# Attention's low parts on VectorE, and the output gate's sums behind each step's own work, in a gated attention and mLSTM layer

## The chip, the core and the metric

The kernel runs on one core of one Trainium2 chip. The metric is the device time of one execution in microseconds (us). The kernel before took 353.72 us, the median of three runs (353.52 to 354.63). TensorE (PE) multiplies matrices; VectorE (DVE), ScalarE (ACT) and GpSimd (POOL) work element by element; SyncE (SP) issues most of the transfers. Each engine works through its own queue in program order and waits where an operand isn't ready.

## The reference, cut to what matters

One layer with 256 tokens and width 1024, all in fp32:

```
ada = c @ w_ada + b_ada;  shift, scale, gate = split(ada, 3)
h  = rmsnorm(x, norm_w) * (1 + scale) + shift
qa ka va za qm km vm zm om ig fg ga gm = split(h @ w_in)
ya = (attention(rmsnorm(qa), rmsnorm(ka), va) * silu(za)) @ w_att_proj
qm, km = silu(causal_conv(qm, km))
hm = rmsnorm(sigmoid(om) * mlstm(qm, km, vm, ig, fg))
ym = (hm * silu(zm)) @ w_ml_proj
y  = sigmoid(ga) * ya + sigmoid(gm) * ym
out = x + gate * (y @ w_out)
```

With 256 tokens the attention has one block and is plain causal attention with a bias.

## The kernel before, in words

**Three passes per product.** PE multiplies in float32r. To keep fp32's precision each operand is split in two: a high part, which ScalarE rounds (`wh`, `hTh`, `yah`, `ymh`), and a low part, the difference, which is a subtraction (`wl`, `hTl`, `yal`, `yml`). PE then makes high by high, high by low and low by high. So every weight that PE uses costs ScalarE one rounding of 128x1024 (L451) and VectorE or GpSimd one subtraction of 128x1024 (L455).

**The stages.** A first stage normalizes x and makes the columns q and part of k. Then one loop over 118 steps does the rest. A step is two of a matrix's eight blocks of 128 input rows, for 512 output columns. The steps are, by the first of each half: ka 0, va 4 and 8, za 12 and 16, qm 20 and 24, zm 28, km 42 and 46, att (attention's projection) 50 and 54, vm 58, ga 72 and 76, om 80, gm 94 and 98, ml (the mLSTM's projection) 102 and 106, out 110 and 114. zm, vm and om have 14 steps and are made by Strassen's scheme with seven products: sums of weight blocks (`sum_forms`) are made before and beside them on VectorE and by accumulating DMAs that POOL issues. A sum may be written over a block (L497), once both subtractions that read the block are done.

**The order in step g** is written out by hand. First the weights of step g+4 are split (`split`, L439 to 456): ScalarE rounds, then VectorE subtracts, or POOL in the ten steps of `pool_lo`, among them 28, 29 (issued at steps 24, 25) and 103, 104 (issued at 99, 100). The ring of `wh` and `wl` has five buffers (HB, L432), so a rounding waits until PE is through with the step five before. Then, at the first step of a chunk, the chunk before is read out of PSUM. Then follow the hooks of the step, in the order in which `at` registered them. Last come PE's matmuls.

**Attention's output.** `att_av` (L746) multiplies probabilities by values for two heads and VectorE multiplies by silu(za) into `yf`; `att_split` (L762) rounds it on ScalarE (`yah`) and subtracts on POOL (`yal`). Heads 4 to 7 have their products at step 22 and their splitting at step 23. PE uses `yah` and `yal` from step 50.

Also at steps 20 to 27: `left_split` and `left_low` (L516, L520) split sums of h for the Strassen products, `sum_forms(zm, 3)` at step 23 issues a DMA from POOL's queue (L481) that adds into the block of zm's weights, `conv` (L778) at steps 24 and 25 reads qm, and `sum_forms(zm, 2)` (L497) at the same steps writes over the block that steps 28 and 29 have read.

**mLSTM's output, steps 94 to 104.** `ml_num` (L870) makes a head's numerator: matmuls, VectorE's product with sigmoid(om) (L883), ScalarE's absolute value and square (L884, L886). `ml_y` (L888) makes the factor of two heads with four small VectorE and three small POOL instructions (L893 to 899). `ml_y2` (L902) multiplies four pieces by it and by silu(zm) (L908). `ml_T` (L911) transposes the result on PE (L919) and splits it into `ymh` (ScalarE, L923) and `yml` (VectorE, L924), which step 102 multiplies. They stand at steps 94, 95, 97 (`ml_num`), 96, 97 (`ml_y`), 97, 98 (`ml_y2`), 99, 100 (`ml_T`).

**The gates.** `ga_mult` (L833) multiplies sigmoid(ga) with attention's projection in halves. `ev_gm` (L837) puts sigmoid(gm) into the same buffer (slot s4) that holds attention's projection. The output gate of `ada` is made by eight sums, `gate_acc` (L942, L944), over weights that `gate_load` brings in four transfers; `gate_write` and `gate_read` (steps 106, 109) spread it over the partitions, for the last read-out (`ev_out`).

A tiny matmul of 128x8 (L1139) stands in five places that `EXTRA` (L301) lists.

Of the kernel before, what the change touches and what calls it, by code (L numbers as in the profile page):

```python
# [9 lines left out]
F32 = mybir.dt.float32  # L10
F32R = mybir.dt.float32r
AF = mybir.ActivationFunctionType
OP = mybir.AluOpType
# [51 lines left out]
def tile_hybrid(ctx: ExitStack, tc: tile.TileContext, x, c, params, params2, rel_t, w_row, ada_mod, ada_gate,  # L65
                w_in, w_att_proj, w_ml_proj, w_out, out):
    nc = tc.nc
# [191 lines left out]
    def some(*what):  # L259
        return lambda k: [mm_row(k, ch, (i,)) for ch, i in what]  # L260
# [19 lines left out]
    for step in P1_STEPS:  # L280
        op, k = step[0], int(step[1])
        if op == "L":
            next_loads(k)
        else:
# [9 lines left out]
                 e=some((0, 0), (0, 1), (0, 2), (1, 0), (1, 1), (1, 2), (2, 0), (2, 1), (3, 0), (3, 1), (2, 2), (3, 2))  # L294
# [3 lines left out]

    chunks = []

    EXTRA = (('za', 0, 0), ('qm', 0, 2), ('km', 0, 0), ('ga', 0, 0), ('ml', 0, 0))  # L301
    STRASSEN = ('zm', 'vm', 'om')

    def seg(kind, src, c0, name, stat=None):
# [29 lines left out]
    def start(name, half=0):  # L334
        return step0[C[name, half]]

    def done(name, half):
        return step0[C[name, half]] + (14 if name in STRASSEN else 4)
# [89 lines left out]
    def aux(shape):  # L428
        return ps.tile(shape, F32, name="aux", bufs=4)
# [5 lines left out]
    for nm, hf in (("qm", 0), ("qm", 1), ("km", 0), ("km", 1)):  # L435
        s = (start("km") if (nm, hf) == ("qm", 1) else done(nm, hf)) + 4
# [23 lines left out]
    def at(step, fn, *a):  # L460
        hooks.setdefault(step, []).append((fn, a))
# [4 lines left out]
    T = {}  # L466
# [295 lines left out]
    def att_split(h0):  # L762
        yf, hs = T["yf", h0], slice(h0, h0 + 2)
        nc.scalar.copy(T["yah"][:, hs], yf)
        nc.gpsimd.tensor_tensor(T["yal"][:, hs], yf, T["yah"][:, hs].bitcast(F32), op=OP.subtract)


    def ev_va(pt, half):
# [226 lines left out]
    for nm in ("qm", "km"):  # L995
        for hf in range(2):
            s = done(nm, hf)
# [4 lines left out]
    for q in range(2):  # L1002
        at(done("za", 0) + 1 + q, att_av, 2 * q)
        at(done("za", 1) + 2, att_av, 4 + 2 * q)
        at(done("za", 0) + 2 + q, att_split, 2 * q)
        at(done("za", 1) + 3, att_split, 4 + 2 * q)
    s = done("km", 0)
    s = done("km", 1)
    at(s + 3, ml_scores, 0)
# [3 lines left out]
    at(start("zm") + 4, gate_init, 0)  # L1013
    at(start("om") - 2, gate_init, 1)
    at(done("ga", 0) + 1, ga_mult, 0)
    at(start("gm") + 5, ga_mult, 1)
    for q, (nm, i, j, k) in enumerate((("km", -9, 4, 6), ("gm", -9, 1, 2), ("ml", -4, -2, -1), ("ml", -3, 0, 2))):
        s = start(nm)
        at(s + i, gate_load, q)
        at(s + j, gate_acc, 2 * q)  # L1020
        at(s + k, gate_acc, 2 * q + 1)
    at(start("ml") + 4, gate_write)
# [6 lines left out]
    for nm in STRASSEN:  # L1029
        s = start(nm)  # L1030
# [8 lines left out]
    for hp in range(2):  # L1039
        s = done("om", hp)  # L1040
        if "om" in STRASSEN:
            for i in range(2):
                at(s + (2 * i + 1, i)[hp], ml_num, 2 * hp + i)
                at(s + (6, 5)[hp], ml_T, 2 * hp + i)
            at(s + (3, 2)[hp], ml_y, hp)
            at(s + (4, 3)[hp], ml_y2, hp)
            continue
        at(s + 1, ml_num, 2 * hp)
        at(s + 2, ml_num, 2 * hp + 1)
        at(s + 3, ml_y, hp)  # L1050
        at(s + 4, ml_y2, hp)
        at(s + 8, ml_T, 2 * hp)
        at(s + 8, ml_T, 2 * hp + 1)

    A = HB - 1
    cons = {}
# [20 lines left out]
    for g in range(NG):  # L1077
# [36 lines left out]
        if ch["kind"] == "str":  # L1114
            p = kp // 2
            o = mmt[ci][(0, 2, 0, 1, 0, 2, 0)[p]]
            for kk in range(2):
                k = 2 * (kp % 2) + kk
# [5 lines left out]
        for kk in range(2):  # L1124
            k = 2 * kp + kk
# [8 lines left out]
            else:  # L1134
                for i in range(4):
                    cs = slice(i * 128, (i + 1) * 128)
                    o = mmt[ci][:, i]
                    if i == 0 and kk == 0 and (ch["name"], ch["half"], kp) in EXTRA:
                        nc.tensor.matmul(aux([128, 8]), wh[:, 0, cs], sh_[:, k, 0:8], start=True, stop=True)  # L1139
# [63 lines left out]
```

## Time and profile before

| | |
|---|---|
| median of three runs | 353.72 us |
| the profiled execution | 353.89 us |
| its span | 352.1 us |
| ScalarE busy | 236.6 us (67%) |
| VectorE busy | 291.3 us (83%) |
| GpSimd busy | 90.9 us (26%) |
| HBM read | 81.89 MB |
| granted TensorE clock | 1.00 throughout |

The span is the profiled execution from its first to its last instruction; 1.8 us lie around it. Times in the profile's timelines count from the span's start. A row of a timeline gives the start, the duration, the engine, the line of the kernel, the operation, what it writes and reads, how many instructions were merged into the row, and in brackets how long the engine had been idle before it and what released it. PE's matmuls are pipelined: they start every 0.11 to 0.24 us, but each lasts longer, so PE's time is read from the starts.

### The profile page before, as it was taken

The numbers are of one execution on the slowest core, as the hardware profiler recorded it, in microseconds if no ns is written. First come the engines' busy times: TensorE is split into PE (matmuls) and PEld (weight loads), VectorE is DVE, ScalarE is ACT, GpSimd is POOL, SyncE is SP. The second block draws the span as 40 slices with busy tenths as digits, with TensorE's granted clock in tenths as the row PEclk, the third lists the DMA queues.
The fourth block names the chain that finished last, engine by engine and source line by source line (L and its number), as shares of the span: only waits on it lengthen the run. The fifth ranks groups of instructions, "written<-read, shape, count | busy, mean of one in ns | idle before, by whom it ended". The sixth has DMA issues, their size and how long they took to land.

```text
span 352.1 us, 6030 instructions
## 1 busy us (share of the span) xinstructions
PE 342.8 (97%) x2313; PEld 312.5 (89%) x2313; DVE 291.3 (83%) x419; ACT 236.6 (67%) x366; POOL 90.9 (26%) x92
## 2 busy tenths in 40 slices
PE   7999999999999999899999999999999999999995
PEld 4987889888999999688999998899988998899885
DVE  3899995898988877999786899998988877698772
ACT  3776787989886946679688657866497554754410
POOL 3940003775101628001453272001000023500000
PEclk9999999999999999999999999999999999999999
DMA  7999999995567699097760973929969369066011
GB/s 275 411 419 421 419 385 345 237 248 240 187 196 280 98 368 236 16 334 323 248 231 2 352 194 63 393 80 360 274 216 400 120 225 374 2 218 202 0 61 60
DMA packets 29534, 83.72 MB, mean 238 GB/s; under 512 B 2109, under 2 KB 5185, under 8 KB 28994
## 3 DMA queue, kind: packets, MB, share of 16 engines
q1 hardware_dynamic: 26944, 78.08, 61.2%
q0 software_dynamic: 2112, 4.19, 7.2%
q10 hardware_dynamic: 450, 1.07, 0.9%
q8 instruction: 18, 0.29, 0.3%
q14 instruction: 10, 0.08, 0.1%
HBM read 81.89 MB, written 1.45 MB: 237 GB/s over the span
## 4 chain that ended last, share of the span: by engine, by line
PE 70%; DVE 10%; DMA 8%; POOL 4%; ACT 3%; issue 3%; SPq 0%; DVEq 0%; POOLq 0%; ACTq 0%
PE mm L1140 13%; PE mm L1142 13%; PE mm L1143 13%; DMA raw<-in_w_row_dram 8%; DVE wl L455 5%; PE pm L186 4%; PE aux L1121 4%; PE aux L1120 4%; PE aux L1122 4%; POOL ms L593 2%; PE mm L1132 2%; PE mm L1131 2%; PE mm L1133 2%; ACT wh L451 1%; PE mm L1154 1%
## 5 line engine op out<-in xcount | busy, mean ns | idle before, releaser
L455 DVE TENSOR_TENSOR wl<-raw,wh 128x1024 fp32r<-128x1024 f32 (+1 forms) x96 | 116.0, 1235 | 19.9 <-ACT wh L451 19.8
L451 ACT CAST wh<-raw 128x1024 fp32r<-128x1024 f32 (+1 forms) x106 | 107.2, 1032 | 28.1 <-PE mm L1142 22.3
L1140 PE MATMUL mm<-hTh,wh 128*128 128x256 f32 x320 | 89.9, 281 | 0.0
L1142 PE MATMUL mm<-hTl,wh 128*128 128x256 f32 x320 | 88.9, 278 | 0.0
L1143 PE MATMUL mm<-hTh,wl 128*128 128x256 f32 x320 | 88.8, 278 | 0.0
L1140 PEld LDWEIGHTS mm<-hTh,wh 128*128 128x128 f32 x320 | 60.3, 188 | 0.1
L1143 PEld LDWEIGHTS mm<-hTh,wl 128*128 128x128 f32 x320 | 60.3, 188 | 0.0
L1142 PEld LDWEIGHTS mm<-hTl,wh 128*128 128x128 f32 x320 | 60.1, 188 | 0.0
L455 POOL TENSOR_TENSOR wl<-raw,wh 128x1024 fp32r<-128x1024 f32 x10 | 25.4, 2606 | 47.2 <-ACT wh L451 47.2
L1131 PE MATMUL mm<-wh,hTh 128*128 128x512 f32 (+1 forms) x64 | 23.8, 372 | 0.0
L1133 PE MATMUL mm<-wh,hTl 128*128 128x512 f32 (+1 forms) x64 | 23.2, 363 | 0.0
L1132 PE MATMUL mm<-wl,hTh 128*128 128x512 f32 (+1 forms) x64 | 23.2, 363 | 0.0
L1121 PE MATMUL aux<-wl,Sh 128*128 128x512 f32 x48 | 19.0, 396 | 1.2 <-DVE wl L455 1.2
L175 DVE TENSOR_TENSOR wrl<-raw,wrh 128x512 fp32r<-128x512 f32 (+1 forms) x24 | 18.2, 780 | 1.1 <-ACT wrh L170 0.8
L1120 PE MATMUL aux<-wh,Sh 128*128 128x512 f32 x48 | 18.7, 390 | 0.0
L1122 PE MATMUL aux<-wh,Sl 128*128 128x512 f32 x48 | 18.7, 389 | 0.0
L1142 PE MATMUL mm<-yml,wh 128*128 128x256 f32 x64 | 17.8, 278 | 0.3 <-DVE yml L924 0.3
L1140 PE MATMUL mm<-yah,wh 128*128 128x256 f32 x64 | 17.8, 279 | 0.0
L170 ACT CAST wrh<-raw 128x512 fp32r<-128x512 f32 (+1 forms) x24 | 15.8, 684 | 3.0 <-DMA raw<-in_w_row_dram 3.0
L1140 PE MATMUL mm<-ymh,wh 128*128 128x256 f32 x64 | 17.8, 277 | 0.0
L1142 PE MATMUL mm<-yal,wh 128*128 128x256 f32 x64 | 17.7, 276 | 0.0
L1143 PE MATMUL mm<-yah,wl 128*128 128x256 f32 x64 | 17.7, 276 | 0.0
(247 smaller groups left out, 815.6 us busy)
## 6 DMA issues: line engine op xcount, KB each, us to landing
raw<-in_w_in_dram SPq DMA_DIRECT2D x36, 1024.0 KB, 7.3
adat<-in_ada_mod_dram SPq DMA_DIRECT2D x16, 512.0 KB, 9.4
gw<-in_ada_gate_dram SPq DMA_DIRECT2D x4, 1024.0 KB, 8.7
raw<-in_w_att_proj_dram SPq DMA_DIRECT2D x4, 1024.0 KB, 8.1
raw<-in_w_ml_proj_dram SPq DMA_DIRECT2D x4, 1024.0 KB, 4.9
raw<-in_w_out_dram SPq DMA_DIRECT2D x4, 1024.0 KB, 4.9
raw<-in_w_row_dram SPq DMA_DIRECT2D x4, 896.0 KB, 12.1
raw<-in_w_in_dram POOLq DMA_DIRECT2D x3, 1024.0 KB, 9.9
```

Source lines behind the costliest of these rows:

```text
L175: e.tensor_tensor(l[:, cs], wrow[k][:, cs], h[:, cs].bitcast(F32), op=OP.subtract)
L451: nc.scalar.copy(h, w)
L455: e.tensor_tensor(l, w, h.bitcast(F32), op=OP.subtract)
L1120: nc.tensor.matmul(o, a, wh[:, kk], start=k == 0 and p in (0, 1, 3), stop=False, skip_group_check=True)
L1121: nc.tensor.matmul(o, a, wl[:, kk], start=False, stop=False, skip_group_check=True)
L1122: nc.tensor.matmul(o, b, wh[:, kk], start=False, stop=k == 3, skip_group_check=True)
L1131: nc.tensor.matmul(o, a, wh[:, kk], start=first, stop=False)
L1132: nc.tensor.matmul(o, a, wl[:, kk], start=False, stop=False)
L1133: nc.tensor.matmul(o, b, wh[:, kk], start=False, stop=last)
L1140: nc.tensor.matmul(o, wh[:, kk, cs], sh_[:, k], start=first and i % 2 == 0, stop=False, skip_group_check=True)
L1142: nc.tensor.matmul(o, wh[:, kk, cs], sl_[:, k], start=False, stop=False, skip_group_check=True)
L1143: nc.tensor.matmul(o, wl[:, kk, cs], sh_[:, k], start=False, stop=last and i % 2 == 1, skip_group_check=True)
```

## The change

Three edits.

First, heads 4 to 7 of attention's output are split at step 22, right behind their product, and their low parts are subtracted by VectorE and no more by POOL. The tiny matmul of qm moves from step 22 to step 23.

Second, the second half of `ga_mult` moves from step 99 to step 94.

Third, the gate's sums 2 to 7 are registered after all other hooks of their step, and some move: sum 2 stays at step 95, 3 goes from 96 to 101, 4 from 100 to 101, 5 from 101 to 102, 6 from 102 to 103, 7 stays at 104. Sums 0 and 1 and all the loads stay.

```
-    EXTRA = (('za', 0, 0), ('qm', 0, 2), ('km', 0, 0), ('ga', 0, 0), ('ml', 0, 0))
+    EXTRA = (('za', 0, 0), ('qm', 0, 3), ('km', 0, 0), ('ga', 0, 0), ('ml', 0, 0))
...
         nc.scalar.copy(T["yah"][:, hs], yf)
-        nc.gpsimd.tensor_tensor(T["yal"][:, hs], yf, T["yah"][:, hs].bitcast(F32), op=OP.subtract)
+        e = nc.gpsimd if h0 < 4 else nc.vector
+        e.tensor_tensor(T["yal"][:, hs], yf, T["yah"][:, hs].bitcast(F32), op=OP.subtract)
...
         at(done("za", 0) + 2 + q, att_split, 2 * q)
-        at(done("za", 1) + 3, att_split, 4 + 2 * q)
+    for q in range(2):
+        at(done("za", 1) + 2, att_split, 4 + 2 * q)
...
-    at(start("gm") + 5, ga_mult, 1)
-    for q, (nm, i, j, k) in enumerate((("km", -9, 4, 6), ("gm", -9, 1, 2), ("ml", -4, -2, -1), ("ml", -3, 0, 2))):
+    for q, (nm, i, j, k) in enumerate((("km", -9, 4, 6), ("gm", -9, 1, 7), ("ml", -4, -1, 0), ("ml", -3, 1, 2))):
         s = start(nm)
         at(s + i, gate_load, q)
+        if q:
+            continue
         at(s + j, gate_acc, 2 * q)
         at(s + k, gate_acc, 2 * q + 1)
...
+    at(start("gm"), ga_mult, 1)
+    for s, j in ((start("gm") + 1, 2), (start("gm") + 7, 3), (start("gm") + 7, 4), (start("ml"), 5),
+                 (start("ml") + 1, 6), (start("ml") + 2, 7)):
+        at(s, gate_acc, j)
```

## The prediction

> **What bounds the kernel now.** I read the page first, then PE's waits, then the chain of waits and each engine's timeline around the two places that the waits point to.
>
> ```profile
> span 352.1 us, 6030 instructions
> PE 342.8 (97%) x2313; PEld 312.5 (89%) x2313; DVE 291.3 (83%) x419; ACT 236.6 (67%) x366; POOL 90.9 (26%) x92
> ```
>
> PE is the bound: 97% of the span, with no piece of its work added or taken away here. So the change can only win what PE stands idle, and lose where it makes PE idle. PE's waits, longest in total first (line that waited, what released it: total, times, longest):
>
> ```profile
> PE aux L1121 <- DVE wl L455: 1.2, 2, 0.6
> PE aux L1120 <- DVE pq L545: 0.6, 1, 0.6
> PE aux L1139 <- ACT ymh L923: 0.5, 1, 0.5
> ...
> PE aux L919 <- DVE omt L908: 0.4, 1, 0.4
> PE mm L1142 <- DVE yml L924: 0.3, 1, 0.3
> PE aux L919 <- ACT wh L451: 0.3, 1, 0.3
> ```
>
> Two stages stand here: zm's Strassen products (L1120, L1121; 1.8 us in three waits) and the way from mLSTM's output into its projection (L919, L1139, L1142; 1.5 us in four waits). An idle row understates a loss, since each matmul's end is modelled. PE's timeline, three matmuls of zm:
>
> ```profile
> 146.36 0.40 PE L1122 MATMUL aux<-wh,Sl 128*128 128x512 f32 x1
> 146.59 0.40 PE L1120 MATMUL aux<-wh,Sh 128*128 128x512 f32 x1
> 147.59 0.49 PE L1121 MATMUL aux<-wl,Sh 128*128 128x512 f32 x1 [0.61 <-DVE wl L455]
> ```
>
> Undisturbed, one starts 0.23 us after the other; here it took 1.00, a loss of 0.77 where the row says 0.61, so 0.16 more. With 0.16 for each wait, zm loses 1.8 + 3 x 0.16 = 2.3 us and the mLSTM stage 1.5 + 4 x 0.16 = 2.1 us: 4.4 us is the most that can be won.
>
> **Attention's splitting and zm.** What it moves: two roundings of ScalarE and two subtractions go forward a step, and the subtractions go from POOL to VectorE. POOL's queue, then ScalarE's, then VectorE's, from their timelines:
>
> ```profile
> 129.98 3.52 POOL L765 TENSOR_TENSOR yal<-yf,yah 128x512 fp32r<-128x512 f32 x2 [9.83 <-ACT yah L764]
> 133.44 1.33 POOL L481 DMA_DIRECT2D raw<-in_w_in_dram  x1
> 134.27 5.30 POOL L455 TENSOR_TENSOR wl<-raw,wh 128x1024 fp32r<-128x1024 f32 x2
> ```
>
> ```profile
> 131.15 1.05 ACT L451 CAST wh<-raw 128x1024 fp32r<-128x1024 f32 x1 [0.73 <-ACT yah L764]
> 132.11 1.01 ACT L789 ACTIVATE qmT<-mm,prm 128x256 f32<-128x256 f32 x2
> 133.99 1.05 ACT L451 CAST wh<-raw 128x1024 fp32r<-128x1024 f32 x1 [0.87 <-PE mm L1142]
> ```
>
> ```profile
> 126.30 0.68 DVE L522 TENSOR_TENSOR Sl<-lsum,Sh 128x512 fp32r<-128x512 f32 x1
> 129.41 1.23 DVE L455 TENSOR_TENSOR wl<-raw,wh 128x1024 fp32r<-128x1024 f32 x1 [2.44 <-ACT wh L451]
> 130.56 1.79 DVE L522 TENSOR_TENSOR Sl<-lsum,Sh 128x512 fp32r<-128x512 f32 x1
> 133.15 2.43 DVE L795 SCALAR_TENSOR_TENSOR qmT<-mm,prm,qmT 128x255 f32<-128x255 f32 x6 [0.81 <-ACT qmT L789]
> 137.24 3.42 DVE L497 TENSOR_TENSOR raw<-t,raw 128x1024 f32<-128x1024 f32 x1 [1.66 <-POOL wl L455]
> ```
>
> The two subtractions hold POOL until 133.50, then comes its DMA issue, and only at 134.27 the two weight subtractions of steps 28 and 29, whose roundings were ready at 132.20 and 135.04. VectorE's sum L497, which overwrites that block, must wait for the first of them (idle 1.66), and then it takes 3.42 us, of which only the last 1.09 lie behind the end of POOL's second subtraction at 139.57: it was held while POOL ran. The same is seen in L522, 1.79 us beside POOL and 0.68 without.
>
> After the change POOL is free long before 132.20. Its first weight subtraction runs from 132.20 and its second from 135.04, where PE's release of the ring (the 0.87 in ScalarE's row) puts the rounding. A subtraction that nothing disturbs is in the row of step 103, from POOL's timeline:
>
> ```profile
> 299.15 2.40 POOL L455 TENSOR_TENSOR wl<-raw,wh 128x1024 fp32r<-128x1024 f32 x1 [4.98 <-ACT wh L451]
> ```
>
> So the first ends at 134.60 and the second at 137.44 (at the mean of the pair, 2.65, at 137.69). L497 still stands behind the second, as VectorE comes to it at 135.58, and ends at 138.53 to 138.78 where it ended at 140.66: VectorE is 1.9 to 2.1 us ahead. I take 2.0. What that is worth is decided by whether VectorE has any other idle time up to PE's last wait there:
>
> ```profile
> 148.60 9.16 DVE L455 TENSOR_TENSOR wl<-raw,wh 128x1024 fp32r<-128x1024 f32 x8
> ...
> 160.55 0.67 DVE L545 TENSOR_TENSOR pq<-pq,aux 128x512 f32<-128x512 f32 x1
> ```
>
> It has none: eight subtractions back to back, no idle time in brackets, up to L545, which released PE's third wait. So the 2.0 us pass through to PE, out of 2.3 lost; the first two waits go and 0.3 stays at L545. **First term: -2.0.**
>
> Its costs: the two subtractions on VectorE, 2 x 0.68 (L522 has the same shape), lie in the 2.44 us of idle time ahead of 129.41. If that cover were gone they would cost at most their 1.36. ScalarE's two roundings now stand ahead of `left_split` and of step 27's rounding; that is ordering inside the same idle time, at nothing. The DMA of POOL's queue (L481, at 133.44) moves forward too, to about when POOL's earlier work ends; it asks for nothing that is made in between, and what it collides with is a rival below. The tiny matmul is one either way: nothing, within ±0.25 (about the spacing of one matmul).
>
> **The gate and the mLSTM stage.** The chain of waits shows where the path runs there (start, the piece's share of the path):
>
> ```profile
> 286.50 1.20 DVE gw L944
> ...
> 294.21 1.68 DVE omt L908 x4
> 295.89 1.15 DVE gat L835
> ...
> 302.41 1.19 DVE gw L944
> ```
>
> and ScalarE's and PE's timelines:
>
> ```profile
> 297.12 1.03 ACT L840 ACTIVATE gmt<-mm 128x1024 f32<-128x1024 f32 x1 [5.25 <-DVE gat L835]
> ```
>
> ```profile
> 291.94 0.30 PE L919 MATMUL aux<-ident,omt 128*128 128x128 f32 x1 [0.26 <-ACT wh L451]
> ...
> 296.30 1.04 PE L919 MATMUL aux<-ident,omt 128*128 128x128 f32 x8
> ```
>
> Between 286 and 304 the path leaves PE and runs through VectorE and ScalarE, and four moved pieces are in it. Sum 2, ahead of heads 0 and 3, and sum 3, ahead of `ml_y`, cost 1.20 each; their removal brings the factors, and with them L908, up to 2.4 us forward. That takes out the two waits of L919 (0.3 + 0.4 + 2 x 0.16 = 1.0), as long as PE's own 1.0 us gain, which makes it ask earlier, is covered: 2.4 against 1.0 and 1.0 again. `ga_mult`'s half (1.15) kept ScalarE idle for 5.25 us at `ev_gm`, with the rounding of step 103 and all of `ymh` behind it in its queue. At step 94 it stands behind nothing that PE waits for; it takes its 1.15 us (plus) from time when VectorE waits for the next rounding, and if that were gone it would cost its 1.15 there, against the 2.4 won behind it. Sum 4 (1.19) stood directly ahead of `yml`, for which PE waited. Together the chain to step 102 loses 2 x 1.20 + 1.15 + 1.19 = 4.7 us; PE needs 2.1. So all 2.1 go, unless a new wait comes.
>
> One can. Step 103's subtraction on POOL, held until 299.15 so far by the late rounding, now starts about when `ml_y2` (L908) of heads 0 and 1 runs, since its rounding then only waits for PE to finish step 98 (291.94 - 0.26 - 0.16 = 291.5): ScalarE's 1.05 later, at some 292.7, POOL starts, and ends 2.40 later at 295.1. The four products take 1.68 and come at about 291.9 (294.21 less 2.3), so the first two are through when POOL starts. Step 100's transposes (296.30 in the row, less the 1.0) begin at 295.3. If the last one or two products wait until POOL ends, at about 295.1, PE stands still for 0.1 to 0.5 us; if none is held, nothing. L908 has both tensor operands in SBUF, as L497 and L522 had, but no row shows it beside a long POOL instruction, so the bounds are 0 and a whole hold (below). I take 0.4, near the middle of what two held products cost. **Second term: -2.1 + 0.4 = -1.7.**
>
> The Trainium skill, page "SBUF — State Buffer", section "Who interferes with whom", says that a VectorE instruction with two SBUF inputs and a GpSimd instruction that reads SBUF exclude one another, and that whichever starts first keeps the shared port for its whole length. L497's 3.42 us agree; by that rule the hold of L908 is certain wherever the two meet, and the sum would lie between this one and the port rival's.
>
> Steps 101 to 104 now hold five sums instead of three, two of them in step 101. They are behind each step's weight subtraction, which is made four steps ahead of PE; in the row
>
> ```profile
> 312.36 1.05 ACT L451 CAST wh<-raw 128x1024 fp32r<-128x1024 f32 x1 [1.67 <-PE mm L1142]
> ```
>
> ScalarE already waits for PE to free the ring, so the splitting runs as far ahead as the ring lets it, and a delay of 2 x 1.20 doesn't reach PE. `gate_write` on SP's queue waits for sum 7, which stays at its step. No moved step issues a DMA.
>
> **The sum.** -2.0 - 1.7 = -3.7 us. The profiled execution (span 352.1, plus what lies around it, in all 353.89) would take 350.2; the median lies 0.17 below the profiled one, so I forecast a median of **350.0 us**. A measurement of this kernel tells about 0.3% (1.06 us) from no change.
>
> **The rivals.**
> - *The port.* The factors come later than worked out, or VectorE loses the first turn, and POOL's subtraction of step 103 holds all four products until about 295.1; they end at 296.8. PE, due at 295.3, waits about 1.3 us instead of 0.4 (the very last product is asked for last). For it speaks how L497 was held; against it, that the products should be two thirds through by then. Time: 350.0 + 0.9 = 350.9. Chance 0.14. By the page's rule above this is the case to expect whenever POOL is first.
> - *One stage only.* If L497 isn't released earlier (POOL's order or DMA issue waits for something else), the first term is 0 and the time 353.72 - 1.7 = 352.0; if the chain through ScalarE only changes its last link, the second is 0 and the time 351.7. For: both stages run near VectorE's limit. Against: each lead is larger than the loss. Chance 0.13 together.
> - *No change.* The waits move to other lines, as the pieces moved stay on the same engine: 353.2 to 354.2. Against: 2 x 1.76 us leave POOL's queue at a place where POOL is late. Chance 0.06.
> - *Slower, through the DMA.* The adding DMA leaves POOL's queue up to 13 us earlier (POOL had been idle for 9.83 us at 129.98, so at 120.15 instead of 133.44), and SP's queue issues the load of the block that L497 adds at about that time. If the two share the transfer engines and the load lands late, L497 and all behind it are late, us for us. The load's issue, and its time to landing (L372):
>
> ```profile
> 121.27 2.57 SPq L372 DMA_DIRECT2D raw<-in_w_in_dram  x2
> ```
>
> ```profile
> DMA to landing us min/median/max: 4.9/7.0/7.4
> ```
>
> It is needed at about 137.4, 16 us after its issue. To end slower by 1.06 the landing must eat both terms: 16 + 3.7 + 1.1 = 21 us after issue, three times the longest row. At 22 us the time is 353.72 + 2.2 = 355.9. Chance 0.05.
>
> **How the numbers follow.** The forecast has what is left, 0.62, with its own range from 349.2 (the whole 4.4 us and a little of restart) to 350.8. The range to hold 8 in 10 takes in the port and the one-stage cases: 349.1 to 352.1; it leaves out no change, slower, and some of the one-stage cases. Faster by over 0.3% (below 352.66): the forecast, the port, and nearly all of the one-stage cases, 0.87. Within 0.3%: 0.08. Slower: 0.05.
>
> **What would show it.** Right: POOL's two subtractions L455 near 132.2 and 135.0; L497 ending near 138.6; no PE wait at L1121, about 0.3 to 0.5 left at L1120 for L545; zm's end about 2 us earlier. `gmt` L840 without an idle time for `gat`; step 103's subtraction on POOL near 292; no PE wait at L1139 or L1142; sums 3 to 7 behind 301 with no PE wait after them. Wrong: L497 starting at the old time; a wait of PE at L919 for L908 of over 1 us (the port); a wait of VectorE for a DMA before L497; PE waits at ml's weights (the sums).

## The result, and the profile after

The changed kernel took 350.12 us (median of four runs, 349.73 to 350.50) against 354.18 us before (four runs, 353.52 to 355.09): a ratio of 0.9884, with a 95% interval from 0.9855 to 0.9912. The profiled execution took 349.88 us with a span of 348.1 us.

PE's waits after the change (line that waited, what released it: total, times, longest):

```profile
PE warm L213 <- POOL ident masks.py:199: 1.4, 1, 1.4
PE aux L1128 <- DVE pq L545: 0.5, 1, 0.5
PE pc L220 <- DMA xnT<-in_c_dram: 0.3, 1, 0.3
```

Of the seven waits in the two stages one is left, at L545. (The diff moves the matmuls' lines by 8: L1120 is now L1128, L1139 is L1147, L1140 to L1143 are L1148 to L1151; `ml_y2` is L909.)

zm first, from the timelines of POOL and VectorE:

```profile
125.42 1.33 POOL L481 DMA_DIRECT2D raw<-in_w_in_dram  x1 [5.78 <-issue]
131.81 2.41 POOL L455 TENSOR_TENSOR wl<-raw,wh 128x1024 fp32r<-128x1024 f32 x1 [5.05 <-ACT wh L451]
134.64 2.40 POOL L455 TENSOR_TENSOR wl<-raw,wh 128x1024 fp32r<-128x1024 f32 x1 [0.42 <-ACT wh L451]
```

```profile
125.99 1.29 DVE L766 TENSOR_TENSOR yal<-yf,yah 128x512 fp32r<-128x512 f32 x2
...
135.02 3.09 DVE L497 TENSOR_TENSOR raw<-t,raw 128x1024 f32<-128x1024 f32 x1
```

POOL's weight subtractions now follow their roundings (the releaser in the brackets is ScalarE's L451), at 131.81 and 134.64. L497 starts at 135.02, without waiting, and is still held while POOL makes the second: it ends at 138.11, of which 1.07 lie behind POOL's end at 137.04. The two subtractions of attention cost VectorE 1.29 us in a place where it had been idle.

Then the mLSTM stage, ScalarE, VectorE and POOL:

```profile
287.22 1.02 ACT L841 ACTIVATE gmt<-mm 128x1024 f32<-128x1024 f32 x1
```

```profile
289.37 3.81 DVE L909 SCALAR_TENSOR_TENSOR omt<-omt,f,zmt 128x256 f32<-128x256 f32 x4
```

```profile
290.22 2.68 POOL L455 TENSOR_TENSOR wl<-raw,wh 128x1024 fp32r<-128x1024 f32 x1 [0.88 <-ACT wh L451]
```

`ev_gm` no longer waits for the gate's product. And the hold that the prediction weighed is there: the four products took 3.81 us instead of the 1.68 before, since POOL's subtraction of step 103 ran beside them; the longest single product is 2.62 us, against 0.48 undisturbed.

Where did the time go? Differences of whole spans mix in the first 120 us, which vary between executions of the same code (PE reaches step 22 at 122.2 to 123.5 us in the kernels below, none of which differs before it). So I cut PE's timeline at the starts of six matmuls: the first of step 22, the first of zm (step 28), km's tiny one (step 42), the first transpose of step 99, the third matmul of ml (step 102), the first of out (step 110), and the span's end. In us:

| | to step 22 | 22-27 | zm | km to 98 | 99 to ml's third | ml | out |
|---|---|---|---|---|---|---|---|
| before | 122.64 | 19.69 | 21.85 | 127.76 | 12.35 | 21.53 | 26.30 |
| after | 122.16 | 19.69 | 19.82 | 127.34 | 10.42 | 22.38 | 26.29 |

zm won 2.03, the mLSTM stage 0.42 + 1.93 = 2.35, and ml, where the change touches nothing that PE does, lost 0.85. The sum is 3.53; the other 0.48 of the spans' difference lies before step 22 and isn't the change's.

The loss in ml has no wait in it. PE's matmuls in ml, before and after:

```profile
305.76 0.28 PE L1140 MATMUL mm<-ymh,wh 128*128 128x256 f32 x1
305.87 0.28 PE L1142 MATMUL mm<-yml,wh 128*128 128x256 f32 x1
305.99 0.28 PE L1143 MATMUL mm<-ymh,wl 128*128 128x256 f32 x1
306.10 0.28 PE L1140 MATMUL mm<-ymh,wh 128*128 128x256 f32 x1
```

```profile
299.90 0.28 PE L1148 MATMUL mm<-ymh,wh 128*128 128x256 f32 x1
300.01 0.28 PE L1150 MATMUL mm<-yml,wh 128*128 128x256 f32 x1
300.13 0.28 PE L1151 MATMUL mm<-ymh,wl 128*128 128x256 f32 x1
300.25 0.28 PE L1148 MATMUL mm<-ymh,wh 128*128 128x256 f32 x1
```

Over a step of 24 they start every 0.1133 us before and every 0.1178 us after, at the same granted clock of 1.00. All of ml keeps its spacing: 192 x 0.0045 = 0.86 us, which is the loss.

### The profile page after: what moved, and what is told of

The parts are those of the page before. It is cut to its first block, busy times and chain, and to the rows that moved or that the text cites. A ratio compares the mean times of both kernels' runs of the same rounds, so it can differ in the third digit from the quotient of the medians.

```text
span 348.1 us, 6032 instructions
## 1 busy us (share of the span) xinstructions
PE 341.7 (98%) x2313; PEld 313.0 (90%) x2313; DVE 293.2 (84%) x421; ACT 237.2 (68%) x366; POOL 88.1 (25%) x90
## 3 DMA queue, kind: packets, MB, share of 16 engines
q10 hardware_dynamic: 450, 1.07, 1.0%
## 4 chain that ended last, share of the span: by engine, by line
PE 74%; DVE 9%; DMA 8%; POOL 4%; issue 2%; ACT 2%; SPq 0%; DVEq 0%; ACTq 0%; POOLq 0%
PE mm L1148 14%; PE mm L1150 14%; PE mm L1151 14%; DMA raw<-in_w_row_dram 8%; PE pm L186 4%; PE aux L1128 4%; PE aux L1130 4%; PE aux L1129 4%; DVE wl L455 4%; POOL ms L593 2%; PE mm L1139 2%; PE mm L1140 2%; PE mm L1141 2%; DVE qmT L796 1%; DVE raw L497 1%
## 5 line engine op out<-in xcount | busy, mean ns | idle before, releaser
L451 ACT CAST wh<-raw 128x1024 fp32r<-128x1024 f32 (+1 forms) x106 | 107.4, 1032 | 29.4 <-PE mm L1150 24.6
L1148 PE MATMUL mm<-hTh,wh 128*128 128x256 f32 x320 | 90.0, 281 | 0.0
L1151 PE MATMUL mm<-hTh,wl 128*128 128x256 f32 x320 | 88.9, 278 | 0.0
L1151 PEld LDWEIGHTS mm<-hTh,wl 128*128 128x128 f32 x320 | 60.4, 189 | 0.0
L1148 PEld LDWEIGHTS mm<-hTh,wh 128*128 128x128 f32 x320 | 60.2, 188 | 0.1
L455 POOL TENSOR_TENSOR wl<-raw,wh 128x1024 fp32r<-128x1024 f32 x10 | 24.6, 2472 | 51.5 <-ACT wh L451 51.5
L1139 PE MATMUL mm<-wh,hTh 128*128 128x512 f32 (+1 forms) x64 | 23.9, 373 | 0.0
L1140 PE MATMUL mm<-wl,hTh 128*128 128x512 f32 (+1 forms) x64 | 23.2, 363 | 0.0
L1128 PE MATMUL aux<-wh,Sh 128*128 128x512 f32 x48 | 18.7, 389 | 0.0
L1148 PE MATMUL mm<-ymh,wh 128*128 128x256 f32 x64 | 18.1, 282 | 0.0
L1151 PE MATMUL mm<-ymh,wl 128*128 128x256 f32 x64 | 18.0, 281 | 0.0
L1148 PE MATMUL mm<-yah,wh 128*128 128x256 f32 x64 | 17.9, 279 | 0.0
```

The lines of the kernel that those rows point to most:

```text
L451: nc.scalar.copy(h, w)
L455: e.tensor_tensor(l, w, h.bitcast(F32), op=OP.subtract)
L1128: nc.tensor.matmul(o, a, wh[:, kk], start=k == 0 and p in (0, 1, 3), stop=False, skip_group_check=True)
L1139: nc.tensor.matmul(o, a, wh[:, kk], start=first, stop=False)
L1140: nc.tensor.matmul(o, a, wl[:, kk], start=False, stop=False)
L1148: nc.tensor.matmul(o, wh[:, kk, cs], sh_[:, k], start=first and i % 2 == 0, stop=False, skip_group_check=True)
```

## The experiments

The stages of all kernels, in us as above, with the time and its ratio to the kernel before on the same chip:

| | median | ratio, 95% interval | zm | km to 98 | 99 to ml's third | ml | out |
|---|---|---|---|---|---|---|---|
| att_only | 351.79 | 0.9943 (0.9930 to 0.9955) | 19.77 | 127.78 | 12.35 | 21.55 | 26.29 |
| gate_only | 352.26 | 0.9954 (0.9941 to 0.9967) | 21.85 | 127.34 | 10.42 | 22.38 | 26.29 |
| mult_only | 354.75 | 1.0026 (1.0017 to 1.0035) | 21.87 | 127.79 | 12.52 | 22.38 | 26.29 |
| sums_only | 352.57 | 0.9958 (0.9943 to 0.9973) | 21.84 | 127.35 | 10.58 | 22.37 | 26.34 |
| pool22 | 350.30 | 0.9899 (0.9874 to 0.9924) | 19.81 | 127.34 | 10.42 | 22.38 | 26.29 |
| vector23 | 350.09 | 0.9881 (0.9865 to 0.9896) | 19.82 | 127.34 | 10.41 | 22.38 | 26.28 |
| step103_vector | 350.28 | 0.9884 (0.9864 to 0.9904) | 19.78 | 127.35 | 10.57 | 22.38 | 26.28 |
| tiny_qm_only | 354.27 | 0.9996 (0.9984 to 1.0007) | 21.75 | 127.78 | 12.35 | 21.55 | 26.29 |
| no_ml_tiny | 349.48 | 0.9866 (0.9851 to 0.9882) | 19.82 | 127.34 | 10.30 | 21.53 | 26.60 |
| ml_tiny_103 | 350.48 | 0.9894 (0.9878 to 0.9909) | 19.81 | 127.35 | 10.30 | 22.39 | 26.29 |
| step29_vector | 349.89 | 0.9867 (0.9844 to 0.9890) | 19.09 | 127.34 | 10.42 | 22.38 | 26.29 |
| both | 349.10 | 0.9849 (0.9831 to 0.9868) | 19.07 | 127.35 | 10.29 | 21.54 | 26.61 |

**Each half alone.** `att_only` is the kernel before with attention's part of the diff; `gate_only` has the rest of it.

> Attention's edit alone (with the tiny matmul of qm at step 23), the gate's work as before. Theory (two stages, each bound by its own chain through VectorE, POOL and ScalarE): zm's steps 28 to 41 fall from 21.85 us to about 19.8, as in the changed kernel, PE's waits at L919, L1139 and L1142 stay at 1.5 us in all; time about 2.0 us below before. Rival (the stages share VectorE's backlog, so one edit relieves both): zm as above and also less than 1.0 us of waits in the mLSTM stage; 2.8 us or more below before.

> The gate's product and sums alone, attention's splitting as before. Theory: zm's steps stay at 21.85 us; PE's waits at L919, L1139 and L1142 go, which wins 2.1 to 2.3 us up to the first products of ml; but ml's 192 matmuls then start 0.118 us apart and not 0.113, as in the changed kernel, which gives back 0.8 us: about 1.4 us below before. Rival (the slower spacing belongs to that one profile, or comes from attention's edit): ml's matmuls at 0.113 us, 2.1 us or more below before.

Both theories hold to 0.1 us by stages: attention's edit wins 2.08 in zm and nothing elsewhere, the gate's edit 2.35 up to ml's third matmul, and it alone brings ml's slower spacing. The two rivals fall. `gate_only` keeps zm's waits:

```profile
PE aux L1127 <- DVE wl L455: 1.2, 2, 0.6
PE aux L1126 <- DVE pq L545: 0.6, 1, 0.6
```

and `att_only` those of the mLSTM stage:

```profile
PE aux L920 <- DVE omt L909: 0.4, 1, 0.4
PE mm L1144 <- DVE yml L925: 0.3, 1, 0.3
PE aux L1141 <- ACT ymh L924: 0.3, 1, 0.3
PE aux L920 <- ACT wh L451: 0.3, 1, 0.3
```

**The gate's edit in its parts.** `mult_only` is the kernel before with

```
-    at(start("gm") + 5, ga_mult, 1)
+    at(start("gm"), ga_mult, 1)
```

and `sums_only` has the sums' new steps, with the product's second half left at step 99.

> Only the second half of the gate's product moves from step 99 to 94; sums and attention as before. Theory: ScalarE no longer idles for it at ev_gm (idle row of 5.25 us gone), so the way to step 102 is short enough and the waits at L1139 and L1142 go (1.1 us with their restarts), while L919's two waits (1.0 us) stay, as sums 2 and 3 still stand ahead of the factors; with ml's matmuls at 0.118 us the time is 0.2 us below before. Rival (sum 4 ahead of yml is the last link): the wait at L1142 stays at about 0.3 us, and ml's matmuls stay at 0.113 us; 0.3 to 0.6 us below before.

> Only the gate's sums 2 to 7 move, the product's second half stays at step 99. Theory: the factors come about 2.2 us earlier and L919's waits go; the chain behind the product at step 99 is earlier by as much, and sum 4 no longer stands in it, so L1139 and L1142 wait no more either, or for less than 0.3 us; with ml's matmuls at 0.118 us about 1.2 us below before, at 0.113 us 2.1 us. Rival (the product at step 99, which holds ScalarE, is the heart of the stage): L1139 and L1142 still wait for 0.6 us or more, about 1.0 us below before.

`sums_only` came out as expected: 0.41 + 1.77 won, 0.84 given back, no wait of PE in the stage. It also shows that moving the product wins PE nothing here. ScalarE of `sums_only`:

```profile
294.96 1.03 ACT L840 ACTIVATE gmt<-mm 128x1024 f32<-128x1024 f32 x1 [4.95 <-DVE gat L835]
```

ScalarE still stands idle for the product (4.95 us, 5.25 before), and PE waits for nothing all the same. The 0.16 us by which the stage is longer than in `gate_only` (10.58 against 10.42) is the spacing of the matmuls of steps 100 and 101: 0.1178 us in `sums_only`, 0.113 in `gate_only`.

`mult_only` missed, and is the most useful run here: slower than before. ScalarE is freed as expected, but the factors are as late as before, so POOL's subtraction of step 103, let go early by the rounding, now comes just ahead of the products. POOL, VectorE and PE of `mult_only`:

```profile
294.23 2.40 POOL L455 TENSOR_TENSOR wl<-raw,wh 128x1024 fp32r<-128x1024 f32 x1
```

```profile
294.31 3.78 DVE L908 SCALAR_TENSOR_TENSOR omt<-omt,f,zmt 128x256 f32<-128x256 f32 x4
```

```profile
292.05 0.30 PE L919 MATMUL aux<-ident,omt 128*128 128x128 f32 x1 [0.28 <-ACT wh L451]
292.75 0.98 PE L919 MATMUL aux<-ident,omt 128*128 128x128 f32 x7 [0.40 <-DVE omt L908]
297.05 0.30 PE L919 MATMUL aux<-ident,omt 128*128 128x128 f32 x1 [0.50 <-DVE omt L908]
297.75 0.98 PE L919 MATMUL aux<-ident,omt 128*128 128x128 f32 x7 [0.40 <-DVE omt L908]
```

The first of the four products is held (it takes 2.60 us), the others come behind it, and the transposes of step 100 (the last two rows) wait for them, in place of the waits at L1139 and L1142 that went. So the stage wins nothing, 12.52 us against 12.35 (steps 100 and 101 ran at the slow spacing, which is about 0.2 us), and the rest of what `mult_only` lost is ml, at the slow spacing: 22.38 against 21.53. The hold on the first product is the prediction's rival of the port. If the gate's product moves, the sums have to move with it, as they bring these four products ahead of POOL; the sums can move alone.

**POOL or VectorE, step 22 or 23.** `pool22` and `vector23` are the changed kernel, the first with both subtractions on POOL, the second with the splitting at step 23:

```
-        e = nc.gpsimd if h0 < 4 else nc.vector
+        e = nc.gpsimd
```

```
-        at(done("za", 1) + 2, att_split, 4 + 2 * q)
+        at(done("za", 1) + 3, att_split, 4 + 2 * q)
```

> The changed kernel, but the low parts of heads 4 to 7 are subtracted by POOL at step 22, and not by VectorE. Theory (what counts is that POOL is free when the rounding for step 28 is ready): the two subtractions run on POOL from about 126 to 129.6 and its DMA issue ends by 131, still ahead of the rounding at 131.7, so L497 ends within 0.2 us of the changed kernel and zm's steps take 19.8 to 20.0 us: the same time as the changed kernel. Rival (VectorE's share counts): zm's steps back to 21 us or more, 1 to 2 us slower than the changed kernel.

> The changed kernel, but attention's second half is split at step 23 as before, with the low parts on VectorE. Theory (POOL's queue is what held L497): POOL has no work of attention left behind step 19, so its two subtractions of weights start with their roundings, and zm's steps take about 19.8 to 20.3 us; the same time as the changed kernel or up to 0.5 us more, as VectorE's 1.3 us now lie at the first part of qm's convolution. Rival (the earlier step counts): zm's steps at 21 us or more.

Both run as fast in zm as the changed kernel (19.81 and 19.82 against 19.82). POOL of `pool22`:

```profile
126.30 2.88 POOL L765 TENSOR_TENSOR yal<-yf,yah 128x512 fp32r<-128x512 f32 x2 [6.39 <-ACT yah L764]
129.10 1.32 POOL L481 DMA_DIRECT2D raw<-in_w_in_dram  x1
132.07 2.41 POOL L455 TENSOR_TENSOR wl<-raw,wh 128x1024 fp32r<-128x1024 f32 x1 [1.65 <-ACT wh L451]
134.90 2.40 POOL L455 TENSOR_TENSOR wl<-raw,wh 128x1024 fp32r<-128x1024 f32 x1 [0.43 <-ACT wh L451]
```

POOL is through 1.65 us before the rounding comes. So neither the engine nor the step is what counts, but that POOL's queue is empty when step 28's rounding is ready; each of the edit's two moves does that by itself.

**The rest of the hold in zm.** L497 was still held for 1.9 us. `step29_vector` gives that one subtraction to VectorE:

```
-        pool_lo.update((s, s + 1))
+        pool_lo.update((s,) if (nm, hf) == ("qm", 0) else (s, s + 1))
```

> The changed kernel, but the subtraction of step 29's weights goes from POOL to VectorE. Theory (L497 is still held while POOL makes it, 3.09 us where 1.21 are its own, and all of zm's start hangs on VectorE): VectorE makes it in 1.21 us, is 0.6 to 0.7 us further at qm's second convolution, and PE's last wait in zm, at L545, goes: 0.5 to 0.65 us faster than the changed kernel. Rival (VectorE is as late with its own subtraction as it was behind POOL's): the wait at L545 stays at 0.4 us or more, the same time as the changed kernel.

```profile
136.06 1.22 DVE L497 TENSOR_TENSOR raw<-t,raw 128x1024 f32<-128x1024 f32 x1
137.19 1.22 DVE L455 TENSOR_TENSOR wl<-raw,wh 128x1024 fp32r<-128x1024 f32 x1
```

Sum and subtraction together take VectorE 2.35 us, less than the held sum took alone (3.09). zm falls from 19.82 to 19.09, and PE has no wait left there. 0.73 by stages is a little over what was expected. The whole time doesn't show it: the executions overlap (349.41 to 350.18 us against 349.73 to 350.50), and the profiled one reached step 22 1.04 us later than the changed kernel's.

**The hold in the mLSTM stage.** `step103_vector` takes step 103's subtraction from POOL.

```
-    pool_lo.update((step0[C["ml", 0]] + 1, step0[C["ml", 0]] + 2))
+    pool_lo.update((step0[C["ml", 0]] + 2,))
```

> The changed kernel, but the subtraction of step 103's weights goes from POOL to VectorE, so that POOL doesn't hold L909 (four products in 3.81 us). Theory (the hold is just covered: the transposes of step 100 ask for the last product when it comes): L909 takes 1.7 us, no PE wait anywhere in the stage as before the edit, the same time as the changed kernel within 0.1 us of the stage's length. Rival (the hold costs PE something that its waits don't show): 0.3 us or more faster.

```profile
289.54 1.67 DVE L909 SCALAR_TENSOR_TENSOR omt<-omt,f,zmt 128x256 f32<-128x256 f32 x4
```

The hold is gone and PE gains nothing; the stage is even 0.15 us longer (10.57), since steps 100 and 101 ran at the slow spacing this time (about 0.2 us). The hold in the changed kernel was covered to the last tenth: it ended at 293.18, and PE came to the last product with the sixth of step 100's eight transposes, at 293.26.

**The spacing in ml.** Three runs: the kernel before with qm's tiny matmul moved alone, and the changed kernel with ml's tiny matmul left out and with it one step later.

```
-    EXTRA = (('za', 0, 0), ('qm', 0, 3), ('km', 0, 0), ('ga', 0, 0), ('ml', 0, 0))
+    EXTRA = (('za', 0, 0), ('qm', 0, 3), ('km', 0, 0), ('ga', 0, 0))
```

> The kernel before with the tiny matmul of qm moved from step 22 to step 23, and nothing else. Theory (the steps from 22 to 27 run at 0.118 us a matmul with it in either place): the way from step 22 to zm stays at 19.69 us, the same time as before. Rival (the place of the tiny matmul sets the spacing here as it does ahead of ml): some of the steps 22 to 27 at 0.113 us, up to 0.65 us faster or none faster and 0.1 us slower.

> The changed kernel without the tiny 128x8 matmul ahead of ml (nothing of the output depends on it). Theory (the spacing of matmuls is a state that a run of equal matmuls keeps until something else comes between; steps 100 and 101 run at 0.113 us, and the tiny matmul ends that): ml's 192 matmuls go on at 0.113 us, 0.8 to 0.9 us faster than the changed kernel. Rival (the new operands of ml, or the missing wait ahead of it, set the spacing): ml at 0.118 us as in the changed kernel, the same time.

> The changed kernel with ml's tiny matmul at step 103 and not at step 102. Theory (the tiny matmul itself sets the spacing anew): step 102 at 0.113 us as steps 100 and 101, steps 103 to 109 at 0.118 us, 0.1 us faster than the changed kernel. Rival (ml's operands set it): all of ml at 0.118 us; second rival: all of ml at 0.113 us, as the tiny matmul only acts where it stands at the first step.

qm's tiny matmul does nothing in either place: the steps before zm take 19.69 us, and the time is the same (zm's 0.10 less is not explained). ml's does. Without it, ml goes on at the 0.1133 us at which steps 100 and 101 ran, and takes 21.53 us again. With it at step 103, step 102 runs at the fast spacing and everything behind the tiny matmul at the slow one. PE of `ml_tiny_103` around it:

```profile
302.57 0.28 PE L1150 MATMUL mm<-yml,wh 128*128 128x256 f32 x1
302.68 0.28 PE L1151 MATMUL mm<-ymh,wl 128*128 128x256 f32 x1
302.80 0.17 PE L1147 MATMUL aux<-ymh,wh 128*128 128x8 f32 x1
302.83 0.36 PE L1148 MATMUL mm<-ymh,wh 128*128 128x256 f32 x1
303.03 0.28 PE L1150 MATMUL mm<-yml,wh 128*128 128x256 f32 x1
```

So the spacing is a state that a run of equal matmuls keeps, and here the tiny matmul put PE into the slow one. ml won 0.85 and the way to it 0.12, but out lost 0.31: PE now comes to out's second half of operands before they are split. The weight loads of PE in `no_ml_tiny`:

```profile
326.43 0.19 PEld L1139 LDWEIGHTS mm<-wh,hTh 128*128 128x128 f32 x1 [0.16 <-ACT hTh L851]
327.15 0.19 PEld L1141 LDWEIGHTS mm<-wh,hTl 128*128 128x128 f32 x1 [0.42 <-DVE hTl L852]
```

**Both further edits.** `both` leaves ml's tiny matmul out and gives step 29's subtraction to VectorE.

> The changed kernel without ml's tiny matmul, and with step 29's subtraction on VectorE. Theory (the two act in stages that share nothing): 0.8 us from ml's spacing and 0.5 to 0.65 us from zm add up, about 1.4 us faster than the changed kernel, 348.7 us, 1.5% below the kernel before. Rival (the spacing of steps 100 and 101 depends on when PE comes there, so the shift in zm can tip it): ml back at 0.118 us, 0.6 us faster than the changed kernel.

349.10 us, 0.9849 of before; by the stages behind step 22 it is 1.39 us faster than the changed kernel, as expected. The forecast 348.7 was missed by 0.4 us; the profiled execution reached step 22 0.60 us later than the changed kernel's, while the two are still the same code.

## Why the prediction was right

It forecast 350.0 us, from two terms of -2.0 and -1.7; 350.12 came. The bound and the two stages were read rightly, and so was the first chain; of the second chain, the share of the gate's product was not. One term was right in size. The other came to -1.50 where -1.7 was forecast, and is that near only because its errors cancel: 0.65 us more was won than it counted, and a loss of 0.85 is not in it. So the closeness of the number is partly luck, also since the start of the kernel alone, up to step 22, varies by over 1 us.

- *First term, -2.0:* 2.03 in zm. POOL's subtractions came at 131.81 and 134.64 (forecast 132.2 and 135.0, in a timeline that ran 0.48 us later), L497 ended 2.55 earlier on the clock and 2.07 within the stage, and the rest of the wait at L545 stayed, 0.47. The theory behind it is shown by `pool22` and `vector23`.
- *The DMA of POOL's queue* was to leave at about 120. It left at 125.42, after 5.78 us in which nothing in the profile is named as the cause; the earlier DMA of that queue, issued at about 115.6, lands 9.6 us later, at 125.2, so it probably waited for that landing. The traces agree: in all eight kernels in which POOL stood idle ahead of this DMA (changed, `att_only`, `vector23`, `step103_vector`, `no_ml_tiny`, `ml_tiny_103`, `step29_vector`, `both`) it left 0.26 to 0.27 us behind that landing, which came between 125.2 and 126.7. No run moves the landing alone. The load that the slower rival feared for was on time: L497 waited for nothing.
- *The covers* held: VectorE's 1.29 us, ScalarE's order and the sums at steps 101 to 104 cost PE nothing.
- *Second term, the leads:* the factors came 2.3 us earlier within the stage, as forecast. But the chain that the prediction shows has three moved pieces and not four (sum 2 ran at 280.71, ahead of it), and PE didn't need the product out of step 99: `sums_only` leaves it there, and PE's waits go.
- *Second term, the 2.1:* up to ml's third matmul 2.35 went. 0.10 of the difference is the tiny matmul, 0.03 us long without the wait ahead of it and 0.13 with it; the rest is within what 0.16 for a restart leaves out.
- *Second term, the 0.4 for the port:* mis-sized. The times were right: on the clock of before, which the changed kernel runs 2.51 us ahead of by then, the products began at 291.9 and POOL at 292.7. The hold came, 2.1 us of it, on the last product. But PE begins with the products that are done, and asked for the last one only when it was there: 0, as `step103_vector` shows. The sentence on the page "SBUF — State Buffer" of the Trainium skill (section "Who interferes with whom") agrees with that pair of runs: L909, with two operands in SBUF, takes 3.81 us beside POOL's subtraction and 1.67 without it. `mult_only` shows the rival itself.
- *Missing from the sum:* ml's spacing, +0.85. The prediction counted what PE stands idle and took the rate of its matmuls for fixed. That there are two rates was in the rows (steps 94 to 98 at 0.118 us and ml at 0.113 before); that ml would change from one to the other was not.

With these corrected the sum is -2.03 - 2.35 + 0.85 = -3.53, where -3.7 was forecast.

## What to carry to other kernels

Follow a wait of the bound engine back to the queue that starts late, and ask only that this queue be empty in time: which engine does the work, and at which of the two steps, made no difference here (zm took 19.81 to 19.82 us in all three ways). When a chain is shortened, check what another engine, let go earlier, will now run beside: moving the gate's product alone only put a hold of the port in place of two waits, and moving the sums, with it or without it, took all of PE's waits in that stage away. Try each piece of a change alone, too: here the gate's product was worth nothing. And cut the bound engine's timeline into stages at fixed instructions: it separates the change from the start's noise, and shows losses that no wait names.

## What the runs showed of the hardware

Runs of the same 128x256 matmul start every 0.1133 us or every 0.1178 us, at the same granted clock, and keep their spacing until other matmuls come between. What decides is only partly known. In eight kernels ml's tiny matmul at step 102, with no wait ahead of or behind it, was followed by the slow spacing, and leaving it out of the changed kernel gave the fast one. Behind the same tiny matmul with waits around it (before, `att_only`, `tiny_qm_only`) ml ran fast, and so did km and ga behind theirs, which follow Strassen's 512-wide matmuls. Steps 100 and 101, which follow eight transposes each time, were fast in some kernels (before, changed, `gate_only`) and slow in others (`att_only`, `mult_only`, `sums_only`, `step103_vector`). What tips them stays open.
